# Issuing TensorE's small fp32 products as groups: the transposes of an attention unit, the masked products and the decay and rate products of two heads

## The chip, the cores and the metric

The kernel runs on one core of a Trainium2 chip. Times are device microseconds (us) of one execution. A time is the median of several runs, here 2107.07 us (three runs, 2104.9 to 2111.75).

## The reference

Two layers over 512 tokens of width 1024. Each layer has a mixer of four branches whose gated outputs are merged, a layer norm, a feed-forward part (dense in layer 0, eight experts with two per token in layer 1) and another layer norm. All is fp32. The change touches two kinds of branch.

Three branches are attentions (sliding window, forgetting, and top-k selected). Cut to what matters, for a head and a block of 128 queries:

```
p = softmax(q @ k.T * 0.125 + mask)     # [128 queries, nk keys]
o = p @ v
```

The recurrent branch (RWKV-7) steps a 64x64 state per head over the tokens:

```
w = exp(-exp(-softplus(-(w0 + tanh(w_lo) @ w_up)) - 0.5))     # decay
a = sigmoid(a0 + a_lo @ a_up)                                 # rate
state = state * w + (state @ -kk) x (kk * a) + v x k
y = state @ r
```

The kernel computes it in chunks of 64 tokens; inside a chunk the steps become products between all pairs of tokens, masked to the earlier ones.

## The kernel before

**Order of work.** The program is written as tile operations. A planner then sets each engine's order ahead of the run, from estimated times: of the instructions whose inputs it expects to be there it takes the one with the highest priority, which is program order unless a block raises it. The recurrent branch stands in such a block (`hot`, L1075), so its instructions go first wherever they are ready, and projections fill TensorE between. On the chip every engine takes its instructions in that fixed order. Products into the same PSUM bank keep their program order. `self.tc.issue_after(ins)` gives the planner one more rule: the instructions traced in its block come behind `ins` on the engine they share; it adds no wait on the chip.

**The mixer** (`mixer`, L348) runs the projections of the recurrent branch, that branch, then value projections, forgetting, sliding-window and selected attention, and the merge. Projections are three fp32r products per block (L111 to L113: high and low halves of weights and activations), most of them 128x512.

**An attention unit** (`attend`, L438) is one or two heads of one block of 128 queries: two where the keys are 256 or fewer, else one. A layer has 40 units, 24 of them with two heads. Logits come into PSUM by L405 and L406 (with masks by L522, L573, L575 or L624), VectorE takes the maximum (L442), ScalarE the exponentials (L451), and VectorE scales each head by its own instruction (L461). Then TensorE turns every 128x128 block of p (L467, fp32, against an identity) into one PSUM bank `ps_t`, in the order: for each key block, head 0 and head 1. ScalarE copies the bank (L470), and `sums` (L473, products at L481) multiplies with v. `sums` already puts the heads' products in alternating order, behind the first one.

**The recurrent branch** (`rwkv`, L764). For each pair g of heads, `rwkv_prep` (L648) makes two K=64 products of 512 columns: the decay's into the PSUM bank `ps_r` from partitions 0 to 63 (L676), the rate's into `ps_y` from partitions 64 to 127 (L677). Each of these banks exists once. ScalarE and VectorE turn `ps_r` into `lw` (L679, L680), then `ps_y` into `a` (L682, L683).

Then four groups of two chunks per layer (the loops over c0 and c1) make the masked products (L817): for each of two chunks and two pairs g, head par takes partitions 64 par to 64 par + 63 of the keys' and the queries' tile, 64 rows by 128 columns, into its own bank: `ps_r` for par 0, `ps_y` for par 1. That is eight products, four per bank. VectorE multiplies each bank with the mask (L822), and transposes of the same chunks (L829, L830) go through `ps_r`. After two such groups their results go through a triangular inverse (`invert16`, L732, and `each` at L848, which alternates the heads in 64x64 products) into the chunk recurrence.

Of the kernel before, what the change touches and what calls it, by code (L numbers as in the profile page):

```python
# [18 lines left out]
P = 128  # L19
# [37 lines left out]
class Net:  # L57
# [380 lines left out]
    def attend(self, s3, nh, nk, nsink=None):  # L438

        nc = self.nc  # L440
        mx = self.bp.tile([P, 8], F32, name="mx", tag="mx", bufs=4)
        nc.vector.tensor_reduce(mx[:, 0:nh], s3, op=OP.max, axis=AX.X)  # L442
        nm = mx[:, 2:2 + nh]
        if nsink is None:
            nc.vector.tensor_scalar(nm, mx[:, 0:nh], -0.125, None, op0=OP.mult)  # L445
        else:
            nc.vector.scalar_tensor_tensor(nm, mx[:, 0:nh], -0.125, nsink, op0=OP.mult, op1=OP.min)
        p = self.bt("pt")
        p3 = p[:, :nh * nk].rearrange("p (h k) -> p h k", h=nh)
        for h in range(nh):  # L450
            nc.scalar.activation(p3[:, h], s3[:, h], AF.Exp, bias=nm[:, h:h + 1], scale=0.125,  # L451
                                 accum_out=mx[:, 4 + h:5 + h])
        den = mx[:, 4:4 + nh]
        if nsink is not None:
            es = mx[:, 6:6 + nh]
            nc.vector.tensor_sub(es, nm, nsink)
            nc.scalar.activation(es, es, AF.Exp)
            nc.vector.tensor_add(den, den, es)
        nc.vector.reciprocal(den, den)
        for h in range(nh):  # L460
            nc.vector.tensor_scalar(p3[:, h], p3[:, h], den[:, h:h + 1], None, op0=OP.mult)  # L461
        pt = self.ps("t")
        nkb = nk // P
        for kb in range(nkb):
            for h in range(nh):
                i = kb * nh + h
                nc.tensor.transpose(pt[:, i * P:(i + 1) * P], p3[:, h, kb * P:(kb + 1) * P], self.ident)  # L467
        ptt = self.bt("pt")
        n = nh * nk
        nc.scalar.copy(ptt[:, :n], pt[:, :n])  # L470
        return ptt

    def sums(self, args):  # L473

        mm = self.nc.tensor.matmul
        first = None
        for ps, v, p, start, stop in args:
            with ExitStack() as st:
                if first is not None:
                    st.enter_context(self.tc.issue_after(first.ins))  # L480
                m = mm(ps, v, p, start=start, stop=stop)  # L481
            first = first or m

    def quad(self, b, nk, logits, kblocks, vcol, o, nsink=None):

# [162 lines left out]
    def rwkv_prep(self, g, r, k, wa):  # L648

        nc, bp = self.nc, self.bp  # L650
        r4 = "p (c a t) -> p c a t"
        kb = [self.bt("rw").rearrange(r4, c=4, a=2) for _ in range(2)]
        ar = [self.bt("rw").rearrange(r4, c=4, a=2) for _ in range(2)]
        pc = bp.tile([P, NCH], F32, name="pc", tag="pc", bufs=2)

        kk, sq = self.bt("rw"), self.bt("rw")
        nc.vector.tensor_scalar(kk, k, self.vcol("k_k", g), None, op0=OP.mult)
        nc.scalar.activation(sq, kk, AF.Square)
        ssq = self.ps("r")
        for tb in range(TB):  # L660
            nc.tensor.matmul(ssq[:, tb * 2:tb * 2 + 2], sq[:, tb * P:(tb + 1) * P], self.halves[:, 0:P:64],
                             start=True, stop=True)
        rn = bp.tile([P, TB * 2], F32, name="rn", tag="rn", bufs=2)
        nc.vector.tensor_scalar(rn, ssq[:, 0:8], 1e-12, None, op0=OP.add)
        nc.gpsimd.tensor_tensor(rn, rn, self.mhalf[:, 0:8], op=OP.pow)
        rnx = sq.rearrange("p (h d) -> p h d", d=64)
        nc.vector.tensor_copy(rnx, rn[:, :, None].to_broadcast([P, 8, 64]))
        rb = self.ps("r")
        for tb in range(TB):
            nc.tensor.matmul(rb[:, tb * P:(tb + 1) * P], sq[:, tb * P:(tb + 1) * P], self.ident, start=True, stop=True)  # L670
        nc.vector.tensor_mul(kk, kk, rb)

        gs = slice(g * P, (g + 1) * P)
        c = math.exp(-0.5)
        ps, pa = self.ps("r"), self.ps("y")
        nc.tensor.matmul(ps, self.wa_up[0:64, gs], wa[0:64], start=True, stop=True)  # L676
        nc.tensor.matmul(pa, self.wa_up[64:128, gs], wa[64:128], start=True, stop=True)  # L677
        lw = self.bt("rw")
        nc.scalar.activation(lw, ps, AF.Tanh, scale=0.5, bias=self.vcol("w0", g, True))  # L679
        nc.vector.tensor_scalar(lw, lw, -0.5 * c, -0.5 * c, op0=OP.mult, op1=OP.add)  # L680
        a = self.bt("rw")
        nc.scalar.activation(a, pa, AF.Tanh, scale=0.5, bias=self.vcol("a0", g, True))  # L682
        nc.vector.tensor_scalar(a, a, 0.5, 0.5, op0=OP.mult, op1=OP.add)  # L683
        L, e_cur = self.bt("rw"), self.bt("rw")
        for tb in range(TB):
            ts = slice(tb * P, (tb + 1) * P)
            nc.vector.tensor_tensor_scan(L[:, ts], self.reset, lw[:, ts], 0.0, op0=OP.mult, op1=OP.add)
        nc.vector.tensor_sub(lw, L, lw)
        e_prev, e_neg = lw, L
        nc.scalar.activation(e_prev, lw, AF.Exp)  # L690
        nc.scalar.activation(e_cur, L, AF.Exp)
        nc.scalar.activation(e_neg, L, AF.Exp, scale=-1.0)
        nc.vector.tensor_copy(pc, e_cur.rearrange("p (c t) -> p c t", t=C)[:, :, C - 1])

        t = sq
        nc.vector.tensor_scalar(t, a, -1.0, self.vcol("k_a", g), op0=OP.add, op1=OP.mult)
        nc.vector.scalar_tensor_tensor(k, t, 1.0, k, op0=OP.add, op1=OP.mult)
        nc.vector.scalar_tensor_tensor(t, kk, -1.0, a, op0=OP.mult, op1=OP.mult)

        def c3(ap):  # L700
            return ap.rearrange("p (c t) -> p c t", t=C)
        for q in range(2):
            for par in range(2):
                rows = slice(64 * par, 64 * par + 64)
                s0, s1 = (0, 1) if par == 0 else (1, 0)
                cs = slice(4 * q, 4 * q + 4)
                for dst, s, x0, x1 in ((ar, s0, kk, e_prev), (ar, s1, r, e_cur), (kb, s0, t, e_neg), (kb, s1, k, e_neg)):
                    nc.vector.tensor_mul(dst[q][rows, :, s], c3(x0)[rows, cs], c3(x1)[rows, cs])
        nc.vector.scalar_tensor_tensor(r, r, self.vcol("r_k", g), k, op0=OP.mult, op1=OP.mult)
        return kb, ar, pc  # L710
# [53 lines left out]
    def rwkv(self, layer, pr):  # L764
        nc, bp, mm = self.nc, self.bp, self.nc.tensor.matmul
# [16 lines left out]
        def KB_(g, ch):  # L782
            return KBt[g][ch // 4][:, ch % 4].rearrange("p a t -> p (a t)")

        def AR_(g, ch):
            return ARt[g][ch // 4][:, ch % 4].rearrange("p a t -> p (a t)")
# [19 lines left out]
        for c0 in (0, 4):  # L806
# [3 lines left out]
            AT = self.bt("rw").rearrange("p (c g t) -> p c g t", c=4, g=2)  # L810
            for c1 in (c0, c0 + 2):
                pss = self.ps("r"), self.ps("y")
                for j in range(2):
                    for g, par in pairs:
                        i = 2 * j + g
                        rows = rows_[par]
                        mm(pss[par][:, i * P:(i + 1) * P], KB_(g, c1 + j)[rows], AR_(g, c1 + j)[rows], start=True,  # L817
                           stop=True)
                am = []
                for par in range(2):  # L820
                    a = self.bt("rw").rearrange("p (i t) -> p i t", i=4)
                    nc.vector.tensor_mul(a, pss[par].rearrange("p (i t) -> p i t", i=4),  # L822
                                         self.m_rw[:, par, None].to_broadcast([P, 4, P]))
                    am.append(a)
                AM.append(am)
                for ch in (c1, c1 + 1):
                    ps = self.ps("r")
                    for g in range(2):
                        nc.tensor.transpose(ps[:, g * P:(g + 1) * P], KB_(g, ch), self.ident)  # L829
                        nc.tensor.transpose(ps[:, 256 + g * P:256 + (g + 1) * P], AR_(g, ch), self.ident)  # L830
                    nc.scalar.copy(KTt[(ch - c0) // 2][:, ch % 2], ps[:, 0:256].rearrange("p (g t) -> p g t", g=2))
                    p4 = ps[:, 256:512].rearrange("p (g e d) -> p g e d", g=2, e=2)
                    nc.scalar.copy(AT[0:64, ch - c0], p4[0:64, :, 0])
                    nc.scalar.copy(AT[64:128, ch - c0], p4[64:128, :, 1])
# [1019 lines left out]
```

## Time and profile before

| | before |
|---|---|
| median of 3 runs | 2107.07 us |
| profiled execution | 2107.6 us, span 2105.9 us, 31148 instructions |
| TensorE products | 2019.7 us busy, 96% |
| TensorE weight loads | 1569.9 us, 75% |
| VectorE | 1366.6 us, 65% |
| ScalarE | 918.0 us, 44% |
| GpSimd | 151.1 us, 7% |
| granted TensorE clock, mean | 0.988 |

The profile is one execution taken by the hardware profiler. PE is TensorE's products, PEld its weight loads, DVE VectorE, ACT ScalarE, POOL GpSimd. Products are pipelined and their ends are modelled, so two neighbouring products' durations overlap; the step from one start to the next tells what a product took. An fp32 product appears as two records, a transpose or an fp32r product as one. L12 is line 12 of the kernel. In the timeline neighbouring records of the same kind are merged, with their count behind an x.

### The profile page before, as it was taken

The numbers are of one execution on the slowest core, as the hardware profiler recorded it, in microseconds if no ns is written. First come the engines' busy times: TensorE is split into PE (matmuls) and PEld (weight loads), VectorE is DVE, ScalarE is ACT, GpSimd is POOL, SyncE is SP. The second block draws the span as 40 slices with busy tenths as digits, with TensorE's granted clock in tenths as the row PEclk, the third lists the DMA queues.
The fourth block names the chain that finished last, engine by engine and source line by source line (L and its number), as shares of the span: only waits on it lengthen the run. The fifth ranks groups of instructions, "written<-read, shape, count | busy, mean of one in ns | idle before, by whom it ended". The sixth has DMA issues, their size and how long they took to land. (4 is left out here: it accounts for less than half of the span.)

```text
span 2105.9 us, 31148 instructions
## 1 busy us (share of the span) xinstructions
PE 2019.7 (96%) x11240; PEld 1569.9 (75%) x11240; DVE 1366.6 (65%) x2732; ACT 918.0 (44%) x1561; POOL 151.1 (7%) x211
## 2 busy tenths in 40 slices
PE   8999999999999999999999999999989999999994
PEld 7767777778888888888767778768877766677663
DVE  5677779844563333236676769844568877788778
ACT  3354543333232222113464553332326666677663
POOL 1020200000000000000011200000000000000043
PEclk9999999999999999999999999999999999999997
DMA  5231213343343334233221213313538988898872
GB/s 159 69 84 39 57 41 90 90 125 96 94 146 99 101 93 133 92 98 115 77 58 43 70 41 90 90 51 95 176 128 308 352 291 304 295 342 306 293 280 82
DMA packets 274976, 294.56 MB, mean 140 GB/s; under 512 B 23852, under 2 KB 203416, under 8 KB 274808
## 3 DMA queue, kind: packets, MB, share of 16 engines
q1 hardware_dynamic: 267736, 273.90, 40.2%
q0 software_dynamic: 7072, 18.49, 2.8%
q8 instruction: 97, 1.59, 0.3%
q14 instruction: 71, 0.58, 0.1%
HBM read 276.74 MB, written 15.60 MB: 139 GB/s over the span
## 5 line engine op out<-in xcount | busy, mean ns | idle before, releaser
L98 ACT CAST whi<-wraw 128x1024 fp32r<-128x1024 f32 (+1 forms) x218 | 228.1, 1046 | 625.4 <-PE ps_mm L112 376.9
L99 DVE TENSOR_TENSOR wlo<-wraw,whi 128x1024 fp32r<-128x1024 f32 (+1 forms) x218 | 265.5, 1218 | 361.2 <-ACT whi L98 355.0
L113 PE MATMUL ps_mm<-xh,wlo 128*128 128x512 f32 (+1 forms) x1288 | 494.9, 384 | 3.1 <-DVE rs L259 3.1
L111 PE MATMUL ps_mm<-xh,whi 128*128 128x512 f32 (+1 forms) x1288 | 496.5, 386 | 0.6 <-ACT whi L98 0.5
L112 PE MATMUL ps_mm<-xl,whi 128*128 128x512 f32 (+1 forms) x1288 | 492.1, 382 | 0.3 <-DVE xl L233 0.3
L113 PEld LDWEIGHTS ps_mm<-xh,wlo 128*128 128x128 f32 x1288 | 243.7, 189 | 49.8 <-DVE wlo L99 3.4
L111 PEld LDWEIGHTS ps_mm<-xh,whi 128*128 128x128 f32 x1288 | 243.8, 190 | 46.5 <-issue 2.6
L112 PEld LDWEIGHTS ps_mm<-xl,whi 128*128 128x128 f32 x1288 | 243.7, 189 | 45.8 <-issue 2.3
L1153 DVE TENSOR_TENSOR wlo<-mwraw,whi 128x1024 fp32r<-128x1024 f32 (+1 forms) x98 | 124.2, 1282 | 17.2 <-ACT whi L1152 16.0
L1152 ACT CAST whi<-mwraw 128x1024 fp32r<-128x1024 f32 (+1 forms) x98 | 95.9, 1005 | 16.0 <-PE ps_t L1503 10.1
L470 ACT COPY bt_pt<-ps_t 128x512 f32<-128x512 f32 (+2 forms) x80 | 41.7, 522 | 85.4 <-PE ps_t L467 84.6
L1153 DVE TENSOR_TENSOR mwlo<-mwraw,mwhi 128x1024 fp32r<-128x1024 f32 (+1 forms) x62 | 71.9, 1175 | 6.9 <-ACT mwhi L1152 6.4
L451 ACT ACTIVATE bt_pt<-ps_s,mx 128x256 f32<-128x256 f32 (+3 forms) x128 | 61.8, 487 | 21.8 <-DVE mx L445 18.0
L260 POOL TENSOR_TENSOR rs<-rs,mhalf 128x1 f32<-128x1 f32 x16 | 13.8, 861 | 724.2 <-DVE rs L259 724.2
L442 DVE TENSOR_REDUCE mx<-ps_s 128x2 f32<-128x512 f32 (+3 forms) x80 | 48.5, 607 | 22.1 <-PE ps_s L406 21.1
L1152 ACT CAST mwhi<-mwraw 128x1024 fp32r<-128x1024 f32 (+1 forms) x62 | 61.0, 999 | 3.2 <-DMA mwraw<-in_exp_w_dram 2.3
L1114 DVE TENSOR_TENSOR bt_pt<-bt_pt,ps_mm 128x512 f32<-128x512 f32 x22 | 15.1, 688 | 70.4 <-PE ps_mm L113 63.0
L467 PE MATMUL ps_t<-ident,bt_pt 128*128 128x128 f32 x272 | 51.5, 283 | 6.0 <-DVE bt_pt L461 4.8
L609 DVE MAX8 m<-bt_pt 128x8 f32<-128x256 f32 (+2 forms) x96 | 53.8, 560 | 2.7
L1153 DVE TENSOR_TENSOR wlo<-ring,whi 128x1024 fp32r<-128x1024 f32 (+1 forms) x45 | 51.5, 1160 | 2.5 <-DMA mwraw<-in_exp_w_dram 1.2
L610 DVE MATCH_REPLACE8 bt_pt<-m,bt_pt 128x256 f32<-128x256 f32 (+2 forms) x96 | 52.1, 543 | 0.0
L111 PE MATMUL ps_mm<-bt_o,whi 128*128 128x512 f32 x128 | 51.2, 400 | 0.4 <-ACT bt_o L511 0.4
(710 smaller groups left out, 4119.1 us busy)
## 6 DMA issues: line engine op xcount, KB each, us to landing
mwraw<-in_exp_w_dram SPq DMA_DIRECT2D x124, 512.0 KB
wraw<-in_w_in_dram SPq DMA_DIRECT2D x106, 512.0 KB
wraw<-in_ffn_w_dram SPq DMA_DIRECT2D x66, 512.0 KB
ring<-in_exp_w_dram SPq DMA_DIRECT2D x60, 512.0 KB
wraw<-in_exp_w_dram SPq DMA_DIRECT2D x32, 512.0 KB
mwraw<-in_exp_w_dram SPq DMA_DIRECT2D x36, 384.0 KB
wraw<-in_w_branch_dram SPq DMA_DIRECT2D x20, 512.0 KB
wraw<-in_w_out_dram SPq DMA_DIRECT2D x16, 512.0 KB
```

The source lines that it names most:

```text
L98: nc.scalar.copy(h, src)
L99: (low or nc.vector).tensor_sub(l, src, h.bitcast(F32))
L111: mm(ps, wh, xh, start=start, stop=False)
L112: mm(ps, wh, xl, start=False, stop=False)
L113: mm(ps, wl, xh, start=False, stop=stop)
L442: nc.vector.tensor_reduce(mx[:, 0:nh], s3, op=OP.max, axis=AX.X)
L451: nc.scalar.activation(p3[:, h], s3[:, h], AF.Exp, bias=nm[:, h:h + 1], scale=0.125, accum_out=mx[:, 4 + h:5 + h])
L467: nc.tensor.transpose(pt[:, i * P:(i + 1) * P], p3[:, h, kb * P:(kb + 1) * P], self.ident)
L609: nc.vector.max(m8, sc[:, :nk])
L610: nc.vector.match_replace(sc[:, :nk], m8, sc[:, :nk], REPL)
L1152: self.chain("hi", lambda: nc.scalar.copy(hi[:, :n], src))
L1153: self.chain("lo", lambda: nc.vector.tensor_sub(lo[:, :n], src, hi[:, :n].bitcast(F32)))
```

## The change

A new method `together` takes a list of functions that each issue one instruction. The first is free; the second comes behind the first; all others come behind the second. Three places use it.

- `attend`: the transposes are issued through it, last head first, and for each head all key blocks.
- `rwkv_prep`: the decay's product, then the rate's.
- `rwkv`: the eight masked products of a group, in the order: for each chunk and pair, par 1 and then par 0.

No instruction is added or removed; each computes what it did.

```diff
-        for kb in range(nkb):
-            for h in range(nh):
-                i = kb * nh + h
-                nc.tensor.transpose(pt[:, i * P:(i + 1) * P], p3[:, h, kb * P:(kb + 1) * P], self.ident)
+
+        def turn(kb, h):
+            i = kb * nh + h
+            return nc.tensor.transpose(pt[:, i * P:(i + 1) * P], p3[:, h, kb * P:(kb + 1) * P], self.ident)
+
+        self.together(*[lambda kb=kb, h=h: turn(kb, h) for h in reversed(range(nh)) for kb in range(nkb)])
...
+    def together(self, *fs):
+
+        after = None
+        for i, f in enumerate(fs):
+            with ExitStack() as st:
+                if after is not None:
+                    st.enter_context(self.tc.issue_after(after.ins))
+                m = f()
+            if i < 2:
+                after = m
...
-        nc.tensor.matmul(ps, self.wa_up[0:64, gs], wa[0:64], start=True, stop=True)
-        nc.tensor.matmul(pa, self.wa_up[64:128, gs], wa[64:128], start=True, stop=True)
+        self.together(lambda: nc.tensor.matmul(ps, self.wa_up[0:64, gs], wa[0:64], start=True, stop=True),
+                      lambda: nc.tensor.matmul(pa, self.wa_up[64:128, gs], wa[64:128], start=True, stop=True))
...
-                for j in range(2):
-                    for g, par in pairs:
-                        i = 2 * j + g
-                        rows = rows_[par]
-                        mm(pss[par][:, i * P:(i + 1) * P], KB_(g, c1 + j)[rows], AR_(g, c1 + j)[rows], start=True,
-                           stop=True)
+
+                def masked(i, par):
+                    g, ch, rows = i % 2, c1 + i // 2, rows_[par]
+                    return mm(pss[par][:, i * P:(i + 1) * P], KB_(g, ch)[rows], AR_(g, ch)[rows], start=True, stop=True)
+                self.together(*[lambda i=i, par=par: masked(i, par) for i in range(4) for par in (1, 0)])
```

## Rows read from the trace of the kernel before

**Rows 1.** The page's first part: busy us, share of the span, instructions.

```profile
PE 2019.7 (96%) x11240; PEld 1569.9 (75%) x11240; DVE 1366.6 (65%) x2732; ACT 918.0 (44%) x1561; POOL 151.1 (7%) x211
```

**Rows 2.** Busy time by stretch; last three numbers: clock, DMA share, GB/s.

```profile
20.00:230.00 210.00, 202.75 (x1392) 156.51 (x1391) 139.57 (x388) 98.98 (x221) 28.36 (x45) 1.00 0.26 70
...
sum 850.00, PE 826.30 PEld 633.46 DVE 612.45 ACT 381.71 POOL 70.92; mean PE 206.58 PEld 158.36 DVE 153.11 ACT 95.43 POOL 17.73
```

**Rows 3.** TensorE's timeline, 202.5 to 204.6: start, duration, instruction.

```profile
202.55 0.39 PE L113 MATMUL ps_mm<-xh,wlo 128*128 128x512 f32 x1
202.78 0.40 PE L111 MATMUL ps_mm<-xh,whi 128*128 128x512 f32 x1
203.11 1.16 PE L817 MATMUL ps_r<-bt_rw 64*128 64x128 f32 x8
204.20 0.50 PE L112 MATMUL ps_mm<-xl,whi 128*128 128x512 f32 x1
204.53 0.39 PE L113 MATMUL ps_mm<-xh,wlo 128*128 128x512 f32 x1
```

**Rows 4.** TensorE's timeline, the first masked products of layer 0.

```profile
91.90 0.49 PE L817 MATMUL ps_y<-bt_rw 64*128 64x128 f32 x2
92.31 0.50 PE L113 MATMUL ps_mm<-xh,wlo 128*128 128x512 f32 x1
...
114.92 1.16 PE L817 MATMUL ps_r<-bt_rw 64*128 64x128 f32 x8
```

**Rows 5.** TensorE's timeline, a decay product.

```profile
68.55 1.12 PE L676 MATMUL ps_r<-bt_rw,wa_up 64*128 64x512 f32 x2
69.60 0.47 PE L427 MATMUL ps_t<-whi,xh 128*128 128x456 f32 x1
```

**Rows 6.** TensorE's timeline, two runs in which the heads alternate.

```profile
255.05 1.15 PE L848 MATMUL ps_r<-bt_rw 64*64 64x64 f32 x32
256.13 0.33 PE L467 MATMUL ps_t<-ident,bt_pt 128*128 128x128 f32 x1
...
441.90 1.09 PE L481 MATMUL ps_o<-bt_pt,bt_v 128*64 128x128 f32 x16
442.92 0.51 PE L112 MATMUL ps_mm<-xl,whi 128*128 128x512 f32 x1
```

**Rows 7.** TensorE's timeline, transposes of three units.

```profile
229.71 0.27 PE L467 MATMUL ps_t<-ident,bt_pt 128*128 128x128 f32 x1
229.74 0.48 PE L113 MATMUL ps_mm<-xh,wlo 128*128 128x512 f32 x1
230.05 0.49 PE L467 MATMUL ps_t<-ident,bt_pt 128*128 128x128 f32 x3
230.30 0.48 PE L111 MATMUL ps_mm<-xh,whi 128*128 128x512 f32 x1
230.61 0.40 PE L112 MATMUL ps_mm<-xl,whi 128*128 128x512 f32 x1
...
237.95 0.39 PE L111 MATMUL ps_mm<-xh,whi 128*128 128x512 f32 x1
238.28 0.30 PE L467 MATMUL ps_t<-ident,bt_pt 128*128 128x128 f32 x1
...
1193.80 0.60 PE L467 MATMUL ps_t<-ident,bt_pt 128*128 128x128 f32 x4
1194.15 0.48 PE L113 MATMUL ps_mm<-xh,wlo 128*128 128x512 f32 x1
1194.47 0.40 PE L111 MATMUL ps_mm<-xh,whi 128*128 128x512 f32 x1
```

**Rows 8.** VectorE's groups (us, mean ns), and L467's idle time on TensorE, times.

```profile
L461 DVE TENSOR_SCALAR bt_pt<-bt_pt,mx 128x256 f32<-128x256 f32 x64 | 20.8, 353 | 0.5
L822 DVE TENSOR_TENSOR bt_rw<-ps_y,m_rw 128x512 f32<-128x512 f32 x8 | 5.4, 680 | 0.0
...
  DVE bt_pt L461: 4.8, 5
```

## The prediction

> **What bounds the kernel now.** I read the page's first two parts, then the busy time by stretch, then TensorE's timeline around each instruction that the diff moves, then the waits. TensorE is busy 96% of the span [rows 1]. In the four stretches that hold attention and the recurrent branch (850 us together) it is busy 826.3 us at a granted clock of 1.00 in the first of them [rows 2]: only 23.7 us of idle time are left there. VectorE and ScalarE have slack (612 and 382 us of 850). So in these stretches the end is set by how long TensorE's queue needs for what is in it, and I price the change in TensorE time: from the start of one instruction to the start of the next on the timeline, not by the durations, which overlap.
>
> **How a run of small fp32 products is priced.** An fp32 product stands in the timeline as two passes. In the stream of projections one 128x512 product follows the next after 0.23 us (202.55 to 202.78). A run of eight passes in it takes 1.09 us to the next start; the product before it holds 0.33 us and the one after it 0.33 us, 0.10 too long each, so the run costs 1.29 us [rows 3]. A run of two costs 0.41 + 0.20 = 0.61 us [rows 4]. So a pass costs (1.29 - 0.61)/6 = 0.11 us and a run 0.39 us whatever its length; a run of six is then 1.06 us.
>
> **Masked products (L817).** Two layers have 8 places of 8 products, 128 passes. Now the y bank's go out when that bank is free, before the r bank's: the timeline holds them as 11 runs of eight passes, 5 of six and 5 of two (one of eight and one of two stand in [rows 3, 4]). They never alternate. Cost: 11 x 1.29 + 5 x 1.06 + 5 x 0.61 = 22.5 us.
>
> After the change the two row halves alternate. What that gives is seen where the kernel alternates already. L481 alternates the output halves: 16 passes of 128 columns take 1.02 us, where 16 x 0.11 would be 1.76. L848 alternates both row and column halves: 32 passes of 64 columns take 1.08 us, where half-length passes in series would be 1.76 too [rows 6]. Both are nearest to passes of opposite halves lying beside each other, with the first and the last alone: 16 passes in 9 slots (0.99 us), 32 short ones in 17 (0.94). No row shows the very form of L817 alternating (64 rows by all 128 columns, two banks), so I bound it: no overlap on one side, the 9 slots on the other; I take the overlap, since L848 also splits the rows.
>
> The second choice is how whole the group is. `together` ties the second product to the first and all others to the second; the first, into y, is free. In all 8 places y starts before r now, by 2.6 to 23 us (91.90 against 114.92 in the first [rows 4]). I expect y's first product to go out alone as a run of two (0.61), and the other seven as one run: 14 passes, r y r y r y r, 8 slots: 8 x 0.11 + 0.39 = 1.27. Eight places x 1.88 = 15.0 us: **7.5 us less**. With the group whole: 9 x 0.11 + 0.39 = 1.38, x 8 = 11.0: 11.5 less. Split and without overlap: 8 x (0.61 + 14 x 0.11 + 0.39) = 20.3: 2.2 less.
>
> **Decay and rate products (L676, L677).** They are four pairs, and now all eight stand alone in the timeline like the one at 68.55, each 1.05 us to the next start [rows 5], with the same 0.20 around it 1.25, so 10.0 us, and a pass (1.25 - 0.39)/2 = 0.43. Paired, r's first pass alone, its second beside y's first, y's second alone: 3 x 0.43 + 0.39 = 1.68, x 4 = 6.7: **3.3 us less**. Without overlap 4 x (4 x 0.43 + 0.39) = 8.4: 1.6 less. Here the first product is r, the late one, and y's bank is free by then, so the pair stays whole.
>
> The Trainium skill ("TensorE: Matmul & The Clock Gate", Part 3, on packing small matmuls) gives another count: tiles of different row groups start about 4 ns apart, so a pair would need the time of one product. By that the pairs would cost 4 x 1.25 = 5.0 us, 5.0 less, and the whole change would gain 1.7 us more than I sum, which stays within the forecast's own range. The rows of L848 and L481 lie above either count of slots and don't tell them apart; I stay with passes in order.
>
> **Transposes (L467).** 48 of the 80 units hold two heads; the timeline has 121 runs of transposes, so about 41 units are split. A split one: 1 transpose 0.03, a projection 0.31, 3 transposes 0.25, a projection 0.31: 0.90 us for four transposes and two projections. A whole one: 0.35 + 0.32, and a plain projection 0.23: 0.90 too [rows 7]. Unlike the 64-row products these switch for nothing. I take **0**. Some runs start 0.1 us later than the stream would let them (238.28, a projection of 0.33 before it [rows 7]); one such start less or more for each of 41 units gives bounds of 4 us either way.
>
> **What comes later, and its cover.** Three things move back: y's mask product on VectorE (0.68 us, eight of them [rows 8]) now follows r's, where it used to be done ahead, 5.4 us on the recurrent chain; `a` of each pair follows `lw`, priced as the same 0.68 us on ScalarE and again on VectorE, 4 x 1.4 = 5.4 us; and a two-headed unit's transposes start when the later head is normalised, 0.35 us after the first [rows 8]. No instruction is added, no DMA moves, no wait between engines is new. Cover for all three is TensorE's supply of projections, 826 of 850 us busy. If it were gone they would cost 5.4, 5.4 and 48 x 0.35 = 16.8 us. I take 0 while it holds; next on TensorE are always the projections that now stand between.
>
> **Sum.** 7.5 + 3.3 + 0 = 10.8 us. The profiled execution took 2107.6 us (span 2105.9, 1.7 around it), so 2096.8; the median is 0.5 lower, 2107.07: about 2096.5, 0.50% faster.
>
> **Rivals.**
> Whole groups: y's first product is held until r is ready. For it: in four places the lead of y is under 3 us. Against: it is a lead in all eight. 11.5 + 3.3 = 14.8, 2092.5.
>
> The change doesn't do what it says: products of 64 rows by 128 columns don't overlap, or other work slips between. Then 2.2 + 1.6 = 3.8, 2103.5. For it: no row of that form alternating. Against: L481 and L848.
>
> Given back: TensorE's order is planned from estimated times, and one moved instruction shifts all that follow. If the 23.7 us of idle time grow by half (12 us) through the 10.8 us of later vector and scalar work, the gain is gone: 2108. For it: VectorE is what the stalled transposes wait for [rows 8]. Against: the chain runs beside projections throughout.
>
> Slower: the transposes' wait for the later head. TensorE takes its queue in order, so behind a transpose that waits stand all projections. Today only 5 transposes stall on VectorE, 4.8 us in all [rows 8]. If the plan puts the group where the first head was ready, each of the 48 units stalls 0.35 us: 16.8 - 10.8 = 6 us slower, 2113. It decides from 31 units on (10.8/0.35). Against: the same risk stands before today's second transposes, and they don't stall.
>
> **Numbers.** Forecast 0.50, whole groups 0.14, no overlap 0.14, given back 0.12, slower 0.10. A difference under 0.3% (6.3 us) can't be told from no change. The first two cases are faster but for small parts: 0.63. No overlap, given back and nearly half of the last lie within: 0.27. Slower by over 0.3%: 0.10. The forecast's own range, with the transposes' bounds, is 2092 to 2101; with whole groups 2088, with the slower side up to 2111: 2088 to 2111.
>
> **What would show it.** L817 as eight runs of two and eight of fourteen, these about 0.9 to 1.1 us to the next start (without overlap 1.6). L676 and L677 in neighbouring rows, 1.3 to 1.5 us together against 2.1. Transposes of a unit in one run, with TensorE's time around them unchanged. Idle time of the four stretches still near 24 us. The forecast is wrong if the alternating runs keep 0.11 us a pass, or if waits on L461, L822 or the recurrent chain grow by several us.

## The result and the profile after

The changed kernel takes 2100.32 us (median of five runs, 2096.98 to 2101.72) where the kernel before takes 2111.75 us on the same chip (2104.9 to 2115.41). The ratio is 0.9947, 95% interval [0.9929, 0.9965]: 0.53% faster. Two further comparisons gave 0.9935 [0.9915, 0.9954] and 0.9941 [0.9924, 0.9959].

The profiled execution took 2099.76 us, span 2098.0, against 2105.9 before, both at a mean granted clock of 0.988: 7.9 us less at the same clock. The five runs of the changed kernel had 0.987 in the mean; the runs of the kernel before had 0.985 in the later comparisons, and beside these five theirs is not on record. A thousandth of clock is some 1.6 us of span by the changed kernel's own spread (2095.3 us at 0.989, 2100.0 at 0.986), so about 3 of the 11.4 us between the medians may come with the clock.

The page's first part and the four stretches of [rows 2], changed kernel:

```profile
PE 2005.5 (96%) x11240; PEld 1561.3 (74%) x11240; DVE 1365.4 (65%) x2732; ACT 916.3 (44%) x1561; POOL 155.1 (7%) x211
...
sum 850.00, PE 819.92 PEld 631.05 DVE 615.29 ACT 382.35 POOL 73.39; mean PE 204.98 PEld 157.76 DVE 153.82 ACT 95.59 POOL 18.35
```

Against [rows 1] TensorE is busy 14.2 us less. The span fell by 7.9 only, so its idle time (span less busy) rose from 86.2 to 92.5 us. In the four stretches it rose from 23.7 to 30.1.

TensorE's timeline of the changed kernel, masked products (now L829); they answer to [rows 3, 4]:

```profile
1155.22 0.49 PE L829 MATMUL ps_y<-bt_rw 64*128 64x128 f32 x2
1155.63 0.51 PE L112 MATMUL ps_mm<-xl,whi 128*128 128x512 f32 x1
...
1161.65 0.40 PE L111 MATMUL ps_mm<-xh,whi 128*128 128x512 f32 x1
1161.98 0.37 PE L829 MATMUL ps_r<-bt_rw 64*128 64x128 f32 x1
1161.99 0.37 PE L829 MATMUL ps_y<-bt_rw 64*128 64x128 f32 x1
1162.19 0.27 PE L829 MATMUL ps_r<-bt_rw 64*128 64x128 f32 x1
1162.20 0.27 PE L829 MATMUL ps_y<-bt_rw 64*128 64x128 f32 x1
...
1162.75 0.38 PE L829 MATMUL ps_r<-bt_rw 64*128 64x128 f32 x2
1163.07 0.33 PE L467 MATMUL ps_t<-ident,bt_pt 128*128 128x128 f32 x1
```

Read the starts in pairs: a pass of r and a pass of y start 0.01 us apart, and the next two 0.11 to 0.21 us later. Fourteen passes take 1.09 us (1161.98 to 1163.07), as long as eight took in [rows 3]. All eight places look like this: one run of two, one run of fourteen.

The decay and rate products (L689, L690), start of the first and all of the second of four pairs, against [rows 5]:

```profile
66.76 0.69 PE L689 MATMUL ps_r<-bt_rw,wa_up 64*128 64x512 f32 x1
...
67.82 0.47 PE L427 MATMUL ps_t<-whi,xh 128*128 128x456 f32 x1
...
87.28 0.69 PE L689 MATMUL ps_r<-bt_rw,wa_up 64*128 64x512 f32 x1
87.28 0.69 PE L690 MATMUL ps_y<-bt_rw,wa_up 64*128 64x512 f32 x1
87.81 0.59 PE L689 MATMUL ps_r<-bt_rw,wa_up 64*128 64x512 f32 x1
87.82 0.59 PE L690 MATMUL ps_y<-bt_rw,wa_up 64*128 64x512 f32 x1
89.18 0.44 PE L808 MATMUL ps_r<-ident,bt_rw 128*128 128x128 f32 x2 [0.77 <-ACT bt_rw L692]
```

Both products start at 87.28. In the first pair, where a projection follows at once, the two take 1.06 us (66.76 to 67.82), the time of one alone. The second pair of each layer is followed by a wait of 0.77 us: the v transposes need bank r, which ScalarE still reads for `lw`.

A second wait comes with the pairs, ahead of the small products of the next norm (`ssq` in `rwkv_prep`; L661 before, L674 after). First the kernel before, then the changed one:

```profile
82.41 1.05 PE L661 MATMUL ps_r<-halves,bt_rw 128*128 128x2 f32 x8
80.62 1.05 PE L674 MATMUL ps_r<-halves,bt_rw 128*128 128x2 f32 x8 [1.34 <-ACT bt_rw L671]
```

From the first decay product of layer 0 to these products it is 13.86 us before (68.55 to 82.41) and 13.86 us after (66.76 to 80.62). Before, the second rate product (71.25) stood in this stretch; now it is gone from there, and 1.34 us of the stretch are idle. In layer 1 the distance is 14.89 us before, with 0.30 us of waiting, and 14.87 after, with 1.49. In all twelve traces of this case both distances are the same within 0.02 us. TensorE's queue does not set them: ScalarE's square (L671) waits for VectorE, which in the changed kernel works without a pause from 69.10 to 79.90.

Transposes of one whole unit, against [rows 7], and what TensorE waits for at all of them, against [rows 8]:

```profile
222.34 0.60 PE L467 MATMUL ps_t<-ident,bt_pt 128*128 128x128 f32 x4
222.70 0.48 PE L113 MATMUL ps_mm<-xh,wlo 128*128 128x512 f32 x1
223.01 0.39 PE L111 MATMUL ps_mm<-xh,whi 128*128 128x512 f32 x1
...
  DVE bt_pt L461: 5.9, 6
```

Four transposes take 0.36 us and the projection after them 0.31, as the whole unit in [rows 7] did. Transposes wait 5.9 us in six places for VectorE's scaling (L461), before 4.8 in five. One of the six, 1.27 us at 438.32, is a unit with one head, so not all of this is waiting for a later head.

### The profile page after: what moved, and what is told of

The parts are those of the page before. It is cut to its first block, busy times and chain, and to the rows that moved or that the text cites. A ratio compares the mean times of both kernels' runs of the same rounds, so it can differ in the third digit from the quotient of the medians.

```text
span 2098.0 us, 31138 instructions
## 1 busy us (share of the span) xinstructions
PE 2005.5 (96%) x11240; PEld 1561.3 (74%) x11240; DVE 1365.4 (65%) x2732; ACT 916.3 (44%) x1561; POOL 155.1 (7%) x211
## 5 line engine op out<-in xcount | busy, mean ns | idle before, releaser
L451 ACT ACTIVATE bt_pt<-ps_s,mx 128x256 f32<-128x256 f32 (+3 forms) x128 | 61.9, 488 | 17.5 <-DVE mx L445 14.2
L442 DVE TENSOR_REDUCE mx<-ps_s 128x2 f32<-128x512 f32 (+3 forms) x80 | 48.5, 607 | 22.5 <-PE ps_s L406 21.8
L467 PE MATMUL ps_t<-ident,bt_pt 128*128 128x128 f32 x272 | 45.1, 281 | 8.5 <-DVE bt_pt L461 5.9
```

Of the source, the lines that this page charges most:

```text
L467: return nc.tensor.transpose(pt[:, i * P:(i + 1) * P], p3[:, h, kb * P:(kb + 1) * P], self.ident)
```

## The experiments

Every kernel was timed beside the kernel before on its chip, and the ratio is to that: 2111.75 us for after, 2112.08 for e1 to e3 and e8, 2113.4 for e4 to e7, 2112.24 for e9 and e10. Busy, idle (span less busy) and clock are of the profiled execution.

| label | median us | ratio to before | TensorE busy | idle | clock |
|---|---|---|---|---|---|
| before | 2111.75 | 1 | 2019.7 | 86.2 | 0.988 |
| after | 2100.32 | 0.9947 [0.9929, 0.9965] | 2005.5 | 92.5 | 0.988 |
| e1_pairs | 2105.6 | 0.9978 [0.9964, 0.9993] | 2014.1 | 88.4 | 0.988 |
| e2_masked | 2102.07 | 0.995 [0.9933, 0.9967] | 2012.4 | 88.0 | 0.987 |
| e3_turns | 2107.84 | 0.9976 [0.9961, 0.9991] | 2019.0 | 85.2 | 0.987 |
| e8_after_again | 2099.66 | 0.9935 [0.9915, 0.9954] | 2006.5 | 92.4 | 0.985 |
| e6_no_turns | 2100.28 | 0.9939 [0.9919, 0.9958] | 2007.0 | 91.2 | 0.988 |
| e4_r_first | 2096.52 | 0.9917 [0.9899, 0.9935] | 1997.2 | 93.8 | 0.991 |
| e5_r_blocks | 2124.03 | 1.0045 [1.0028, 1.0063] | 2016.7 | 105.2 | 0.981 |
| e7_no_turns_r_first | 2110.44 | 0.9978 [0.9966, 0.9989] | 2006.3 | 102.5 | 0.985 |
| e9_r_first_again | 2096.53 | 0.9935 [0.9915, 0.9956] | 1996.9 | 94.6 | 0.992 |
| e10_after_third | 2098.65 | 0.9941 [0.9924, 0.9959] | 2007.0 | 91.2 | 0.986 |

My theory was that opposite row halves overlap; the rival, that only the number of runs and their switches matter. Two kernels tell them apart: the same eight runs of sixteen passes each, alternating or not.

**e4_r_first.** Alternating, the late bank first.

```diff
-for i in range(4) for par in (1, 0)])
+for i in range(4) for par in (0, 1)])
```

> As the changed kernel, but the masked products of a group begin with the r bank's (par 0 before par 1), so the free first product is the late one and the group goes out whole: eight runs of 16 passes, no run of two. Theory of overlap (products of opposite row halves run beside each other, both passes of one beside both of the other): a run still takes 8 pass slots, 1.09 us to the next start as the runs of 14 do in the changed kernel, and the eight runs of two go, 8 x 0.61 = 4.9 us of TensorE time less than the changed kernel. By the steps on TensorE's timeline the masked products then cost 8 x 1.29 = 10.3 us against 22.5 before. Time: 2100.3 - 4.9 = about 2095, 0.8% under before if idle time stays. Rival, the gain is from fewer runs and their switches, the order in a run does not matter: same time as the run with the halves in blocks.

Its TensorE timeline, first, second and last pair of a run of sixteen and what follows:

```profile
203.02 0.37 PE L829 MATMUL ps_r<-bt_rw 64*128 64x128 f32 x1
203.02 0.37 PE L829 MATMUL ps_y<-bt_rw 64*128 64x128 f32 x1
203.23 0.27 PE L829 MATMUL ps_r<-bt_rw 64*128 64x128 f32 x1
203.24 0.27 PE L829 MATMUL ps_y<-bt_rw 64*128 64x128 f32 x1
...
203.90 0.27 PE L829 MATMUL ps_r<-bt_rw 64*128 64x128 f32 x1
203.91 0.27 PE L829 MATMUL ps_y<-bt_rw 64*128 64x128 f32 x1
204.11 0.33 PE L467 MATMUL ps_t<-ident,bt_pt 128*128 128x128 f32 x1
```

Sixteen passes take the same 1.09 us as fourteen, and no run of two is left. Both are eight steps: sixteen are eight pairs, and of the fourteen the last two, both of r, stand alone behind six pairs. Busy time is 8.3 us below the changed kernel's, more than the 4.9 expected, but at a clock of 0.991 against 0.988.

**e5_r_blocks.** The same runs, one bank's products before the other's.

```diff
-for i in range(4) for par in (1, 0)])
+for par in (0, 1) for i in range(4)])
```

> As the run with r first, but inside the group all four products of the r bank come before all four of the y bank: the same eight runs of 16 passes, no alternation. Theory of overlap: only the border of the two blocks overlaps, a run takes 1.9 to 2.0 us to the next start instead of 1.09, 8 x 0.8 = 6.5 to 7 us more than with alternation, about 2102. Rival of switches: 1.09 us a run and the same time as with alternation.

The run in the same place:

```profile
203.48 0.82 PE L829 MATMUL ps_r<-bt_rw 64*128 64x128 f32 x5
204.04 0.37 PE L829 MATMUL ps_y<-bt_rw 64*128 64x128 f32 x1
204.14 0.27 PE L829 MATMUL ps_r<-bt_rw 64*128 64x128 f32 x1
204.25 0.27 PE L829 MATMUL ps_y<-bt_rw 64*128 64x128 f32 x1
204.25 0.27 PE L829 MATMUL ps_r<-bt_rw 64*128 64x128 f32 x1
204.36 0.27 PE L829 MATMUL ps_y<-bt_rw 64*128 64x128 f32 x1
204.37 0.27 PE L829 MATMUL ps_r<-bt_rw 64*128 64x128 f32 x1
204.47 0.72 PE L829 MATMUL ps_y<-bt_rw 64*128 64x128 f32 x5
205.12 0.28 PE L535 MATMUL ps_s<-m_swa,identb 128*128 128x256 bf16 x1
```

1.64 us against 1.09, with the same group, the same switches and the same count of passes. That refutes the rival: the order inside the run is worth 0.55 us, and only six passes around the border overlap. In the seven other places the next start comes 1.94 us after the run's, 0.23 of it a wait for r's mask product (L834), as behind the run at 115.88:

```profile
117.82 0.33 PE L841 MATMUL ps_r<-ident,bt_rw 128*128 128x128 f32 x1 [0.23 <-DVE bt_rw L834]
```

So the run itself takes 1.64 to 1.71 us, and the eight cost about 5 us more than alternating ones, not the 6.5 to 7 expected. With 0.20 us around each run the masked products come to about 15 us here, as in the changed kernel: issuing each group whole, in two blocks, saves about 7 of the 22.5 us, and alternating it some 5 more.

About 2102 us was expected, and this kernel is 27 us slower than e4. The rest does not lie in the runs: there are 11 us more idle time and a clock of 0.981 against 0.991. It has two long waits at the end of attention in each layer (2.20 us before 441.2, 2.65 before 450.64, and the same again before 1403.17 and 1412.4), which e7 shows more clearly. Why the planner's order came out so was not isolated.

**e1_pairs, e2_masked, e3_turns.** One part of the change at a time, the two others as before the change.

```diff
# e1: only this
+        self.together(lambda: nc.tensor.matmul(ps, self.wa_up[0:64, gs], ...), lambda: nc.tensor.matmul(pa, ...))
# e2: only this
+                self.together(*[lambda i=i, par=par: masked(i, par) for i in range(4) for par in (1, 0)])
# e3: only this
+        self.together(*[lambda kb=kb, h=h: turn(kb, h) for h in reversed(range(nh)) for kb in range(nkb)])
```

> Only the decay and rate products are paired, all else as before the change. Theory of the pair as two slots (measured in the changed kernel: both products of a pair start together and the pair takes 1.06 us to the next start): 4 x 1.25 = 5.0 us of TensorE time less than before. For g = 1 the v transposes after the pair wait 0.77 us for lw on ScalarE in the changed kernel, twice, so 3.5 us less in time, 0.17%. My prediction's three slots a pair: 3.3 us less in TensorE time. Rival, the planner's new order moves more than the pair gives: TensorE's idle time differs from the 57.9 us of before by more than 3.5 us and the time follows that.

> Only the masked products go out as in the changed kernel (y's first alone, the other seven alternating), pairs and transposes as before the change. Theory of overlap: eight runs of two and eight of fourteen, 15.1 us against 22.5 before, 7.4 us of TensorE time less, 0.35% if idle time and clock stay. Rival of the planner's new order: idle time or clock eats it, time within 0.2% of before.

> Only the transposes are grouped. My theory: no TensorE time gained or lost by the runs themselves, time as before within 4 us, with TensorE's idle time at transposes up from 5 to 8 us. Rival that a two-headed unit stalls for the later head: up to 16 us slower. Rival that grouping saves a switch per unit: 41 units x 0.1 = 4 us faster.

> The changed kernel again, on the same chip as the three single parts. Adding the parts: 5.0 + 7.4 + 0 = 12.4 us of TensorE time less than before; with the 6 us more of TensorE idle time that its profile showed, 6 to 12 us less in time, 0.3% to 0.6%. If the parts' times add up to this, they act apart; if not, the planner's order for each kernel is a cause of its own.

The page's first line of each (e1, e2, e3), to be set against [rows 1]:

```profile
PE 2014.1 (96%) x11240; PEld 1566.3 (74%) x11240; DVE 1365.2 (65%) x2732; ACT 918.5 (44%) x1561; POOL 153.7 (7%) x211
```

```profile
PE 2012.4 (96%) x11240; PEld 1564.0 (74%) x11240; DVE 1365.5 (65%) x2732; ACT 915.4 (44%) x1561; POOL 151.7 (7%) x211
```

```profile
PE 2019.0 (96%) x11240; PEld 1569.3 (75%) x11240; DVE 1368.1 (65%) x2732; ACT 917.5 (44%) x1561; POOL 151.1 (7%) x211
```

In TensorE's busy time the parts add up: 5.6 for the pairs, 7.3 for the masked products, 0.7 for the transposes, 13.6 together, where the whole change has 14.2. In time they hardly do: 0.22%, 0.50% and 0.24% less make 0.96%, and the changed kernel beside them has 0.65% [0.46, 0.85], a gap not much wider than the intervals. The pairs and the masked products came out as expected, a little more in time.

Of the pairs' 5.6 us, though, 4.1 stand against two waits that every trace with the pairs has and none without: 1.5 us behind the pairs, and 2.8 to 2.9 us before the norm's small products where the others have 0.3. In e1 the idle time rose by 2.2 us all the same, since other waits are shorter in its order. How much of its 0.22% is the pairs' own is therefore not shown.

The transposes alone are 0.24% faster [0.09, 0.39], 2 to 8 us where I had allowed 4; their idle time at L461 went down to 3.8 us in this order, not up. The kernel before has one long wait at the end of attention, shown with e7 below, and e3's trace has none. That can be the cause, but was not tested by itself.

**e6_no_turns, e7_no_turns_r_first.** The changed kernel and e4, with the transposes as before the change.

```diff
-        self.together(*[lambda kb=kb, h=h: turn(kb, h) for h in reversed(range(nh)) for kb in range(nkb)])
+        for kb in range(nkb):
+            for h in range(nh):
+                ...
```

> As the changed kernel, with the transposes issued as before the change (key block, then head, nothing grouped). My theory: the transposes' grouping gives no TensorE time (0.90 us for four transposes and two projections both ways), and the stalls of transposes on the later head are its only effect (7.8 us of TensorE idle time at transposes after, 5.2 before): same time as the changed kernel or up to 4 us faster, 2096 to 2100. Rival, the grouped transposes carry a part of the gain: slower than the changed kernel by that part.

> Both of the others together: masked products r first, transposes as before the change, decay and rate products paired. If the transposes' grouping gives nothing and whole groups of masked products save the runs of two, this is the fastest: 22.5 - 10.3 = 12.2 us and 5.0 us of TensorE time less than before, 2107 - 17 = 2090 with idle time unchanged, 2096 if idle time grows by 6 us as it did in the changed kernel. If the grouped transposes carry gain, slower than the run with r first and grouped transposes.

e6 has 0.9939 on its chip, the changed kernel 0.9935 to 0.9947 in three comparisons: beside the other two parts the transposes give nothing that can be measured. e7, expected to be the fastest, is 14 us slower than e4. Its timeline shows where most of it lies; the end of selected attention in layer 0:

```profile
440.03 1.09 PE L467 MATMUL ps_t<-ident,bt_pt 128*128 128x128 f32 x4 [3.37 <-DVE bt_pt L461]
441.79 1.98 PE L481 MATMUL ps_o<-bt_pt,bt_v 128*64 128x128 f32 x16 [0.68 <-ACT bt_pt L470]
444.16 0.80 PE L111 MATMUL ps_mm<-bt_o,whi 128*128 128x512 f32 x1 [0.39 <-ACT bt_o L522]
```

and its busy time by stretch around it (clock third from the right):

```profile
428.00:436.00 8.00, 8.00 (x52) 5.92 (x51) 3.58 (x12) 3.74 (x9) 0.00 (x0) 1.00 0.25 66
436.00:444.00 8.00, 3.72 (x23) 2.48 (x21) 2.54 (x5) 2.80 (x6) 0.00 (x0) 0.70 0.59 186
444.00:452.00 8.00, 7.84 (x31) 6.43 (x32) 1.96 (x4) 0.42 (x3) 0.00 (x0) 0.88 0.85 242
```

The last unit has one head and nothing beside it in the queue: TensorE waits 3.37 us for VectorE, then 0.68 and 0.39. In the eight us that hold the first wait the granted clock is 0.70 and in the next 0.88, so part of them ran at the lower level, 1.2 GHz; four transposes take 1.09 us in duration instead of 0.60. Idle 4.4 us, and for the clock at most 3.4 us (8 x 0.30 + 8 x 0.12), or 2 us if only TensorE's busy time is counted (3.72 x 0.30 + 7.84 x 0.12): 6 to 8 us. e7 has it in both layers (again at 1395.07). In e4 the same units wait 1.26 us instead of 3.37 and the clock stays at 1.00, so this accounts for about 8 to 11 of the 14 us. The kernel before has it in layer 1 alone:

```profile
1395.65 1.09 PE L467 MATMUL ps_t<-ident,bt_pt 128*128 128x128 f32 x4 [2.76 <-DVE bt_pt L461]
1397.42 1.97 PE L481 MATMUL ps_o<-bt_pt,bt_v 128*64 128x128 f32 x16 [0.67 <-ACT bt_pt L470]
1399.76 0.80 PE L111 MATMUL ps_mm<-bt_o,whi 128*128 128x512 f32 x1 [0.37 <-ACT bt_o L511]
```

The changed kernel has a short one in layer 0 (1.27, 0.68 and 0.39 us, the clock full) and none in layer 1. e1 has a long one in layer 0 (2.75 us before 441.92) and e2 in layer 1 (2.75 before 1390.01); e3 and e6 have none above 1.26 us.

**e9_r_first_again, e10_after_third.** e4 and the changed kernel unaltered, on one chip.

> The version with r first in the masked products, all three parts grouped, once more, on the same chip as the changed kernel. Its masked runs take 8 x 0.61 = 4.9 us less TensorE time than the changed kernel's; on another chip its ratio to before was 0.9917 against 0.9935 and 0.9947 for the changed kernel. If the lone runs of two are real cost: 3 to 5 us faster than the changed kernel here too. If the planner's order decides: no difference outside the intervals.

> The changed kernel beside the version with r first: ratio to before 0.993 to 0.995 as in its two earlier comparisons.

2096.53 against 2098.65 us, and intervals that overlap: no gain over the changed kernel that these runs can tell, though its busy time is 10.1 us lower here too (1996.9 against 2007.0, at clocks of 0.992 and 0.986). e9's profiled execution, 2093.25 us, was the fastest of its six, so these two busy times overstate the difference.

## Why the prediction was right

The forecast was 2096.5 us, 0.50% faster, with 2088 to 2111; it became 0.53%. (Its own sum, 2107.07 - 10.8, gives 2096.3.) By its steps:

- **Masked products: right in mechanism, and in size by a count that was right by luck.** Forecast 15.0 us after the change, 7.5 less: eight runs of two and eight of fourteen, 1.27 us each. Measured eight and eight, 0.61 and 1.09 + 0.20 = 1.29: 15.2 us, 7.3 less; in e2's busy time 7.3. That y's first product goes out alone held in all eight places. e4 and e5 show that the alternation of a whole group is worth about 5 us, beside the 7 of issuing it whole. But I had the halves lie shifted by one pass, the first and the last alone; the trace has them start together. For fourteen passes both make eight slots, for sixteen the trace has eight (1.29 us in e4) and not my nine (1.38).
- **Decay and rate products: right in mechanism, the size too small.** I let a pair take three slots, r's second pass beside y's first. Both passes lie side by side: 1.06 + 0.20 = 1.26 us a pair instead of 1.68, and four pairs save 10.0 - 5.0 = 5.0 us, not 3.3 (e1's busy time: 5.6). The Trainium skill's count ("TensorE: Matmul & The Clock Gate", Part 3), by which products of different row groups start about 4 ns apart and a pair needs the time of one, was the right one: the trace has both at 87.28. My rows could have told it. Against the 1.02 and 1.08 us of L481 and L848 I set bare slots, 0.99 and 0.94 us, and left out what a run costs beside its passes, of whose 0.39 us all but the 0.20 around it lie inside. With these 0.19 us, 9 and 17 slots are 1.18 and 1.13 us, and 8 and 16 slots 1.07 both, nearer to what the rows show.
- **Transposes: right on TensorE's time** (0.36 us for four, as before), and nothing measurable beside the other parts (e6). Alone they are 0.24% faster, which the runs themselves don't explain.
- **The cover: the step that held only in part.** I took everything that comes later at nothing, since TensorE's queue sets the end. Idle time rose by 6.3 us, and 4.1 us of new waits come with the pairs. Two of 0.77 us stand behind them: both products of a pair end together, and `lw` is then still to be made. Another 2.5 us stand before the norm's small products: there the branch's VectorE work sets the time, and TensorE's queue does not, so the time of the rate product taken out came back as a wait. Of the pairs' 5.0 us about 1 is left after these waits. The waits of transposes on L461 rose by 1.1, but in e1 and e2, where transposes stand as before, they are 6.0 and 6.2 us too. The rest goes with the planner's new order. The shorter runs make 12.3 us by their steps (7.3 + 5.0); busy time fell by 14.2, and the span by 7.9.
- **Given back** came about at half its size: 6 us of idle time against 12. **Slower, by the later head** did not: 1.1 us more of waits on L461, not 16.8. **Whole groups** needed the other bank first (e4) and then brought little in time.

What the sum did not hold: layer 0's mixer is 3.0 us shorter (its layer norm's transposes start at 576.7 instead of 579.7), layer 1's then another 5.9 (1516.5 instead of 1525.4). In layer 1 the kernel before also loses the unhidden last unit and its clock. That the change removes this is chance as far as these runs go: e1 and e2, with one of its parts each, have it once, and e7, with the same pairs and another order of the masked products, has it twice. So part of the agreement between forecast and result is luck: the pair's larger gain and the removed wait made up for the idle time that I had left out. How much each planner's order contributes is still open.

## What to carry to other kernels

Price small products by the step from start to start, per run and per pass: here a run of 64-row fp32 products among 128-row projections cost 0.39 us whatever its length, while a run of transposes cost nothing, so grouping pays for the one and not for the other. Products on opposite row halves overlap only around the places where the halves meet in the queue; alternate them, and issue the one that is ready last first, or the early one goes out alone. Time taken off TensorE counts only where TensorE sets the time: 2.5 us of what the pairs saved came back as waits for VectorE's chain. Where a planner orders the whole program, one unhidden wait with its loss of clock (6 to 8 us here) is not much less than a local gain of 0.5%, so look for those in both traces before crediting the edit.

## What the hardware showed that I had not expected

- A later product on the other row half overtakes earlier ones. In e5 eight passes of r stand in the queue before y, yet y's first pass starts at 204.04, before r's sixth (204.14); all eight runs show this. So between the two row halves TensorE's starts do not keep the fixed order that the section on the order of work tells of.
- Passes of the two halves go in step: 0.01 us apart, in pairs 0.11 us apart, so 16 passes take the time of 8 (1.09 us).
- After a wait of 3.37 us in e7 the granted clock was 0.70 and 0.88 in the two stretches of 8 us around and behind it; after one of 1.69 us in the changed kernel (at 1073.12) it was 0.79 in 1072 to 1080. The wait of 1.27 us at 438.32 left it at full level, but in e10, the same kernel, the same wait (before 438.82) was followed by 0.79 in 440 to 448. So in these traces the length of the wait does not decide alone.
